# Splitting the first load of a NaN-ignoring row maximum into two loads, over even and odd partitions

## The chip, the cores and the metric

The kernel runs on one core of a Trainium2 chip. The metric is the device time of one execution in microseconds (us), of which the median over several runs is given. A profile is one further execution recorded by the hardware profiler; its engines are called DVE (VectorE), ACT (ScalarE), POOL (GpSimd) and SP (SyncE, which issues the DMAs).

## The reference

The input has 32 x 2048 rows of 2048 float32 values, one in ten of them NaN. The output is the maximum of each row, NaNs left out:

```python
x = np.random.randn(32, 2048, 2048).astype(np.float32)
x[np.random.rand(32, 2048, 2048) < 0.1] = np.nan
return np.nanmax(x, axis=-1).astype(np.float32)
```

The input is 537 MB and is read once; the output is 0.26 MB.

## The kernel before

The 65,536 rows are dealt to 128 partitions, so each partition has 512 rows. They are worked through in 74 tiles. A full tile takes seven rows from every partition (128 x 57,344 bytes, 7168 KB); the first tile, tile 0, takes one row of each partition (128 x 8 KB, 1 MB), and the last tiles are cut into smaller loads. Three buffers `xt0`, `xt1`, `xt2` hold tiles in turn.

Each piece of a tile passes four stages:

1. A load from HBM into `xt`, issued by SP (L269 for tile 0, L466 for all others).
2. ACT reads the upper 16 bits of every value and writes a 16-bit key into a buffer `kt` (L282, `kt<-xt`). The function is a Prelu, whose two slopes send NaN patterns to other keys than numbers.
3. POOL (L292) or, for some pieces, ACT (L282, `xt<-kt`) turns the key back into the upper half of the value in place, which leaves a very low number where a NaN stood.
4. DVE takes the maximum of each row (L299) into `acc`.

Rows of nothing but NaN are found at the end of each part of `acc` (L305, L319), and six stores (L533) bring the result out.

The order of the work is written out by hand. A table `TILES` says how each tile is cut for loads, keys, writing back and maxima. All of it stands in a critical section, in which the class `Order` places the semaphore waits: `order.add` gives an instruction its waits and lets it count up a semaphore. Loads count up one of `LANES = 14` semaphores in turn, and a load waits for the one that used its lane before, and for the DVE maximum that frees its buffer. A full load into a buffer can therefore be issued when the tile three places before it is done.

The critical section starts with a small synchronisation: SP passes it (L276, L582), and ACT and POOL wait for that before their first instructions, ACT's table load and a memset by POOL. The load of tile 0 is issued ahead of the section (`HEADS = 1`): a loop before `tc.tile_critical()` makes its `dma_start` and keeps the instruction in `heads`; inside the section, `order.add` for tile 0 takes this instruction from the list rather than issuing one, so that it gets its lane. The destination is given a dependency offset beyond the buffer (`dep_tracking_offset`), and the instruction is put in `no_tile_sem_insts`, so that the framework adds no waits of its own. The first key pass of ACT (128 x 2048, tile 0) waits for this lane. The loads of tiles 1 and 2 have no earlier user of their buffers and are issued at once after it.

Of the kernel before, what the change touches and what calls it, by code (L numbers as in the profile page):

```python
# [9 lines left out]
D = 2048  # L10

Q = D // 4
# [55 lines left out]
WIDE = 7  # L68
# [5 lines left out]
LEAD = 128  # L74

HEADS = 1

LANES = 14

# [13 lines left out]
def joints(keys, backs, reds):  # L93


    parts = []
    pieces = []
    at = end = step = 0
    for n, wait in backs:
        end += n  # L100
        while at < end:
            at += keys[step]
            step += 1
        if wait is None or wait >= 0:
            parts.append((end - n, end, wait is not None, step + (wait or 0), len(pieces)))
        pieces.append(n)
    needs = []
    done = 0
    for n in map(abs, reds):
        over = [i for i, p in enumerate(parts) if p[0] < done + n and p[1] > done]  # L110
        done += n
        pools = [i for i in over if not parts[i][2]]
        acts = sorted((i for i in over if parts[i][2]), key=lambda i: parts[i][3])
        if pools and acts and parts[pools[-1]][3] > parts[acts[-1]][3]:
            acts = []
        needs.append(pools[-1:] + acts[-1:])
    pairs = {}
    for need in needs:
        if len(need) == 2 and all(sum(i in n for n in needs) == 1 for i in need):
            both = tuple(parts[i][4] for i in need)  # L120
            for i in both:
                pairs[i] = both
    return pairs
# [62 lines left out]
def kernel(  # L186
# [15 lines left out]
    nc = tc.nc  # L202
    P = nc.NUM_PARTITIONS
# [14 lines left out]
    for tiles in GROUPS:  # L218
        at = 0
# [8 lines left out]
    firsts = [  # L228
        nc.alloc_sbuf_tensor(f"xt{i}", [P, WIDE * D], i32).ap() for i in range(HEADS)
    ]  # L230
# [6 lines left out]
    xts = firsts + [  # L237
        sing.tile([P, WIDE * D], i32, name=f"xt{i}") for i in range(HEADS, BUFS)
    ]
# [10 lines left out]
    groups = []  # L250
# [12 lines left out]
    order = Order(nc)  # L263
    heads = []
    for number in range(HEADS):
        (c,) = TILES[number][0]
        gi, base = place[number]
        to = xts[number][:, 0 : c * Q]
        head = nc.sync.dma_start(  # L269
            out=dataclasses.replace(to, dep_tracking_offset=to.offset + P * WIDE * D),  # L270
            in_=groups[gi][0][:, base : base + c * Q],
        )
        tc.no_tile_sem_insts.add(head.ins.name)
        heads.append(head)

    with tc.tile_critical() as section:  # L276

# [52 lines left out]
        lanes = [[] for _ in range(LANES)]  # L330
        turn = 0
# [43 lines left out]
        def freed(*ks):  # L375

            uses = [(back, then, e) for k in ks for back, ((_, then), e) in kfree[k].items()]
            counts = [e[1] for _, _, e in uses if e[0] == "pool"]
            deps = []
            for back, then, e in uses:  # L380
                if back == "act" and order.count["act"] >= then:
                    e = ("act", then)
                if back != "pool" or e[0] == "pool" or all(v < then for v in counts):
                    deps.append(e)
            return deps
# [39 lines left out]
        def find_part(i):  # L425
            gi, lo, hi = spans[i]
            first = groups[gi][2]
            acc = accs[:, first + lo : first + hi]
            deps = [done_at[PARTS[i][2]]]
            if PARTS[i][3] == "dve":  # L430
                none = nones[:, 0 : hi - lo]
                ready[i] = find("dve", nc.vector, deps, acc, none, ALU.bitwise_or)
            else:
                none = late[:, 0 : hi - lo]
                ready[i] = find("pool", nc.gpsimd, deps, acc, none, ALU.add)

        for number, (loads, chunks, reds) in enumerate(TILES):
            keys = [k for ks, _ in chunks for k in ks]
            fresh = {}
            step = 0  # L440
            for ks, bs in chunks:
                assert sum(ks) * Q <= KEYS
                assert sum(ks) == sum(b[0] if isinstance(b, tuple) else b for b in bs)
                fresh[step] = sum(ks) * Q
                step += len(ks)
            backs = [b for _, bs in chunks for b in bs]
            backs = [b if isinstance(b, tuple) else (b, None) for b in backs]
            assert sum(loads) == sum(keys) == sum(b for b, _ in backs) == sum(map(abs, reds))
            pairs[number] = joints(keys, backs, reds)
            for i, part in enumerate(PARTS):  # L450
                if part[3] == number:
                    find_part(i)
            gi, base = place[number]
            xg = groups[gi][0]
            xt, before = xts[number % BUFS], free[number % BUFS]
            assert number < BUFS or state["tile"] > number - BUFS
            landed = []
            at = 0
            for c in loads:
                c *= Q  # L460
                e = order.add(
                    "sp",
                    nc.sync,
                    lambda: heads[number]
                    if number < HEADS
                    else nc.sync.dma_start(  # L466
                        out=xt[:, at : at + c], in_=xg[:, base + at : base + at + c]
                    ),
                    before + lanes[turn],
                    lane=f"load{turn}",  # L470
                    step=16,
                )
                lanes[turn] = [e]
                turn = (turn + 1) % LANES
                landed.append((at, at + c, e))
                at += c
            end = at
            at = lo = part = 0
            for step, c in enumerate(keys):
                c *= Q  # L480
                here = [l for a, b, l in landed if a < at + c and b > at]
                kold = []
                if used + fresh.get(step, 0) > KEYS:
                    key = (key + 1) % NKEYS
                    used = 0
                    assert all(h[3] != key for h in held)
                    assert all(q[2] != key for v in half.values() for q in v)
                    kold = freed(key, (key + 1) % NKEYS) if number in EARLY and at + c == end else freed(key)
                    kfree[key] = {}
                e_key = act(  # L490
                    kold + here,
                    out=kts[key][:, used : used + c],
                    in_=xt[:, at : at + c].bitcast(i16)[:, 1::2],
                    func=ACT.Prelu,
                    bias=EDGE,
                    scale=-1.0,
                    alpha=float(TOP - LOW) / (EDGE - NAN),
                )
                used += c
                at += c  # L500
                for h in held:
                    h[-1] -= 1
                for h in [h for h in held if h[-1] <= 0]:
                    held.remove(h)
                    write(*h[:-1], "act")
                while backs and lo + backs[0][0] * Q <= at:
                    n, wait = backs.pop(0)
                    n *= Q
                    kp = kts[key][:, used - (at - lo) : used - (at - lo) + n]
                    if wait is not None and wait > 0:  # L510
                        held.append([number, lo, lo + n, key, kp, e_key, part, wait])
                    else:
                        who = "pool" if wait is None else "act" if wait == 0 else "dve"
                        write(number, lo, lo + n, key, kp, e_key, part, who)
                    lo += n
                    part += 1
                if number == len(TILES) - 1 and at == end:
                    for h in held:
                        write(*h[:-1], "act")
                    held.clear()  # L520
                maxima(number)
            assert lo == end
# [5 lines left out]
        for (gi, lo, hi), e in zip(spans, ready):  # L528
            _, og, first, _ = groups[gi]
# [4 lines left out]
                    out=og[:, lo:hi], in_=accs[:, first + lo : first + hi].bitcast(i32),  # L534
# [3 lines left out]
                lane="store",  # L538
                step=16,
# [47 lines left out]
```

## Time and profile before

| what | value |
|---|---|
| median of 3 runs | 1251.33 us (1251.32 to 1251.34) |
| the profiled execution | 1251.31 us |
| its span in the profile | 1249.7 us |
| DMA, mean over the span | 430 GB/s |
| busy time of POOL, DVE, ACT | 1158.9, 1109.7, 980.1 us |
| issue of the first load (L269) | at 0.72 us, takes 0.39 us |
| tile 0 usable (first key pass of ACT) | 5.49 us |

The span goes from the first instruction to the last; the execution's time contains 1.6 us around it. In the rows of the profile L269 is a line of the kernel, "xt<-in_x_dram" is what is written and what is read (buffer numbers left out), and "x62" is a count. The DMA figures are of the 16 DMA engines together. A row of the chain of waits has start, length and what ran or was waited for; "issue" is time in which nothing that the profile shows was waited for, and "SPq" is the queue of SP.

### The profile page before, as it was taken

What the parts mean: (1) busy time and instruction counts of PE and PEld (TensorE: products, weight loads), DVE (VectorE), ACT (ScalarE), POOL (GpSimd) and SP (SyncE); (2) the same over time, 40 slices, a digit from 0 to 9 for tenths busy, and PEclk for the clock granted to TensorE, in tenths of its full rate; (3) what the DMA queues carried; (4) which work ended last, traced back from release to release, by engine and by line L of the source; (5) the groups of instructions that cost most, each with busy time, mean ns of one, the idle gap of its engine ahead of it and who ended that gap; (6) DMA issues with size and microseconds to landing.
All of it is one profiled execution on the core that took longest, in us unless ns stands there. A gap on an engine that the chain in (4) does not pass through costs nothing.

```text
span 1249.7 us, 920 instructions
## 1 busy us (share of the span) xinstructions
DVE 1109.7 (89%) x184; ACT 980.1 (78%) x286; POOL 1158.9 (93%) x256
## 2 busy tenths in 40 slices
DVE  0888889888889888888988888988898999999999
ACT  3777777777777777777777777799877799999998
POOL 2999999999999999999999999967999987999998
DMA  9999999999999999999999999999999999999997
GB/s 415 441 428 424 441 441 437 415 441 441 439 426 428 441 439 433 422 439 441 439 426 428 441 439 435 426 433 441 439 428 426 441 437 431 425 436 428 429 428 313
DMA packets 16854, 537.19 MB, mean 430 GB/s; under 512 B 2640, under 2 KB 2640, under 8 KB 5200
## 3 DMA queue, kind: packets, MB, share of 16 engines
q1 hardware_dynamic: 16848, 537.14, 99.5%
q14 instruction: 6, 0.05, 0.0%
HBM read 536.87 MB, written 0.26 MB: 430 GB/s over the span
## 4 chain that ended last, share of the span: by engine, by line
POOL 34%; DVE 30%; DMA 26%; ACT 9%; issue 1%; SPq 0%
POOL xt L292 34%; DVE acc L299 30%; DMA xt<-in_x_dram 26%; ACT kt L282 7%; ACT xt L282 2%; POOL late L305 0%; POOL acc L319 0%; SPq L269 0%; SPq L466 0%; DVE none L305 0%; DVE acc L319 0%; SPq L582 0%; SPq L276 0%
## 5 line engine op out<-in xcount | busy, mean ns | idle before, releaser
L292 POOL TENSOR_SCALAR xt<-kt 128x3584 int16<-128x3584 uint16 (+10 forms) x241 | 1153.9, 4788 | 84.5 <-ACT kt L282 69.3
L299 DVE TENSOR_REDUCE acc<-xt 128x4 f32<-128x8192 f32 (+4 forms) x182 | 1109.4, 6148 | 137.5 <-POOL xt L292 130.6
L282 ACT ACTIVATE kt<-xt 128x3584 uint16<-128x3584 int16 (+10 forms) x252 | 913.9, 3663 | 262.3 <-DMA xt<-in_x_dram 225.0
L282 ACT ACTIVATE xt<-kt 128x512 int16<-128x512 uint16 (+7 forms) x32 | 68.6, 2145 | 0.7
L305 POOL TENSOR_SCALAR late<-acc 128x112 int32<-128x112 f32 (+1 forms) x5 | 2.8, 558 | 0.4
L319 POOL TENSOR_TENSOR acc<-acc,late 128x112 int32<-128x112 int32 (+1 forms) x5 | 2.0, 397 | 0.4
L282 ACT ACT_TABLE_LOAD x1 | 1.3, 1283 | 1.3 <-SPq L276 1.3
L325 POOL MEMSET scalars<- 128x1 f32 x1 | 0.1, 98 | 1.0 <-SPq L276 1.0
L568 POOL MEMSET const-float32-0.0<- 128x1 f32 x1 | 0.1, 98 | 0.2 <-issue 0.2
L282 ACT ACTIVATE scalars<-scalars 128x1 f32<-128x1 f32 x1 | 0.2, 203 | 0.0
L305 DVE TENSOR_SCALAR none<-acc 128x7 int32<-128x7 f32 x1 | 0.2, 169 | 0.0
L319 DVE TENSOR_TENSOR acc<-acc,none 128x7 int32<-128x7 int32 x1 | 0.2, 161 | 0.0
L568 POOL MEMSET const-bfloat16-1.0<- 128x1 bf16 x1 | 0.1, 101 | 0.0
L568 POOL MEMSET const-uint8-127<- 128x1 uint8 x1 | 0.1, 101 | 0.0
L568 POOL MEMSET const-float32-1.0<- 128x1 f32 x1 | 0.1, 98 | 0.0
## 6 DMA issues: line engine op xcount, KB each, us to landing
xt<-in_x_dram SPq DMA_DIRECT2D x62, 7168.0 KB, 22.6
xt<-in_x_dram SPq DMA_DIRECT2D x2, 4096.0 KB, 19.4
xt<-in_x_dram SPq DMA_DIRECT2D x2, 3584.0 KB, 25.6
xt<-in_x_dram SPq DMA_DIRECT2D x5, 1280.0 KB, 29.4
xt<-in_x_dram SPq DMA_DIRECT2D x4, 1536.0 KB, 24.2
xt<-in_x_dram SPq DMA_DIRECT2D x2, 3072.0 KB, 26.3
xt<-in_x_dram SPq DMA_DIRECT2D x1, 5632.0 KB, 19.5
xt<-in_x_dram SPq DMA_DIRECT2D x2, 2816.0 KB, 24.8
```

Of the source, the lines that this page charges most:

```text
L282: lambda: nc.scalar.activation(**kw),
L292: lambda: nc.gpsimd.tensor_scalar(**kw),
L299: return order.add("dve", nc.vector, lambda: do(**kw), deps)
L305: lambda: engine.tensor_scalar(out=none, in0=acc, scalar1=NONE, scalar2=float(0x00800000), op0=ALU.is_equal, op1=ALU.mult,),
L319: lambda: engine.tensor_tensor(out=bits, in0=bits, in1=none, op=op),
L325: e_top = order.add("pool", nc.gpsimd, lambda: nc.gpsimd.memset(top, EDGE), [])
L568: nc = _bacc.Bacc("TRN2", target_bir_lowering=False, num_devices=1)
```

## The change

The load of tile 0 is issued as two loads. The first takes the even partitions (rows 0, 2, 4 ... of `to`), the second the odd ones, 64 rows of 8 KB each. Both are still issued ahead of the critical section, one behind the other on SP. Inside the section each part gets a lane of its own, so tile 0 uses two of the 14 lanes, and all later loads take the next lane in turn. `landed` gets an entry for each part over the same columns, so that ACT's key pass of tile 0 waits for both. No other instruction is changed; the lines below the edit move by a few numbers (the issue of the head stands at L274, that of the other loads at L469).

```diff
+PHASES = ((0, 2), (1, 2))
+
...
-        head = nc.sync.dma_start(
-            out=dataclasses.replace(to, dep_tracking_offset=to.offset + P * WIDE * D),
-            in_=groups[gi][0][:, base : base + c * Q],
-        )
-        tc.no_tile_sem_insts.add(head.ins.name)
-        heads.append(head)
+        heads.append([])
+        for first, step in PHASES:
+            part = to[first::step]
+            head = nc.sync.dma_start(
+                out=dataclasses.replace(
+                    part, dep_tracking_offset=part.offset + P * WIDE * D
+                ),
+                in_=groups[gi][0][first::step, base : base + c * Q],
+            )
+            tc.no_tile_sem_insts.add(head.ins.name)
+            heads[number].append(head)
...
-                e = order.add(
-                    "sp",
-                    nc.sync,
-                    lambda: heads[number]
-                    if number < HEADS
-                    else nc.sync.dma_start(
+                issues = [
+                    lambda: nc.sync.dma_start(
                         out=xt[:, at : at + c], in_=xg[:, base + at : base + at + c]
-                    ),
-                    before + lanes[turn],
-                    lane=f"load{turn}",
-                    step=16,
-                )
-                lanes[turn] = [e]
-                turn = (turn + 1) % LANES
-                landed.append((at, at + c, e))
+                    )
+                ]
+                if number < HEADS:
+                    issues = [lambda head=head: head for head in heads[number]]
+                for issue in issues:
+                    e = order.add(
+                        "sp",
+                        nc.sync,
+                        issue,
+                        before + lanes[turn],
+                        lane=f"load{turn}",
+                        step=16,
+                    )
+                    lanes[turn] = [e]
+                    turn = (turn + 1) % LANES
+                    landed.append((at, at + c, e))
```

## The prediction

> **What bounds the kernel now.** I read the page's strips and queue line first, then the chain of waits that ended last, then the first 25 us of the timeline, and last the busy time of short stretches around the first load.
>
> ```profile
> DVE 1109.7 (89%) x184; ACT 980.1 (78%) x286; POOL 1158.9 (93%) x256
> ...
> DMA  9999999999999999999999999999999999999997
> ...
> q1 hardware_dynamic: 16848, 537.14, 99.5%
> ```
>
> POOL is the busiest compute engine with 93%, but the DMA strip is at nine tenths in every slice but the last: the stream of loads never pauses. The next rows (stretch, its length, busy time and count for DVE, ACT and POOL, clock, DMA share, GB/s) give its pace.
>
> ```profile
> 100.00:1000.00 900.00, 804.16 (x108) 681.93 (x165) 862.83 (x163) 1.00 1.00 434
> 1100.00:1230.00 130.00, 130.00 (x42) 125.41 (x60) 120.48 (x43) 1.00 1.01 430
> ```
>
> A full tile of 7168 KB, that is 7.34 MB, takes 7.34 / 434 = 16.9 us at this pace. So the time at which a tile is usable is the start of the stream plus the bytes ahead of it. The chain of waits says the same from the other side (start, length, what):
>
> ```profile
> 0.72 0.39 SPq L269
> 1.11 0.04 issue
> 1.15 0.01 SPq L276
> 1.17 0.06 issue
> 1.22 0.03 SPq L582
> 1.25 0.13 issue
> 1.38 0.33 SPq L466
> 1.71 0.05 issue
> 1.77 37.60 DMA xt<-in_x_dram
> ...
> 1032.58 22.14 DMA xt<-in_x_dram
> 1054.72 0.02 issue
> ...
> 1068.06 0.02 issue
> 1068.08 169.86 DVE acc L299 x52
> 1237.94 0.01 issue
> 1237.95 8.93 DVE acc L299 x4
> ```
>
> It begins at the very instruction that the change splits (L269), goes through the second full tile, which lands at 1.77 + 37.60 = 39.37, comes back to loads up to the landing at 1054.72, and ends in DVE without a gap from 1068.08 on. The load that lands at 1054.72 was issued 22.14 us before, 5.2 us more than the 16.9 us its bytes need, so it queued behind the load before it: the stream, not its issue, set that landing. Hence whatever moves the start of the stream by d moves the end by d. I take this one to one. A chain shows the last releaser alone, and POOL at 93% could have a second chain almost as late; but POOL's data come from the same stream, so it moves along.
>
> **The change part by part.** The head load (tile 0, 128 rows of 8 KB, 1.05 MB) becomes two loads of 64 rows each, 0.52 MB. It adds one DMA issue on SP, one semaphore lane used at the start, and one wait on ACT, whose first key pass now needs both parts.
>
> (1) The added issue on SP. Its price is the duration of an issue:
>
> ```profile
> L269 SPq DMA_DIRECT2D xt<-in_x_dram x1: 385/385/385, 0.7 to 0.7; - x1
> L466 SPq DMA_DIRECT2D xt<-in_x_dram x2: 333/376/420, 1.4 to 1.8; - x2
> ```
>
> These are minimum, median and maximum in ns, of L466 those before 2 us; a 64-row issue is not in the trace, and I take 0.39 us, between 0.33 and 0.42. Everything that SP has behind it moves by that: the entry of the critical section (L276, L582), for which ACT and POOL wait, and the first two L466 issues, from 1.38 to about 1.77 and from 1.77 to 2.16.
>
> ```profile
> 1.34 1.28 ACT L282 ACT_TABLE_LOAD   x1 [1.34 <-SPq L276]
> 1.38 0.10 POOL L325 MEMSET scalars<- 128x1 f32 x1 [0.95 <-SPq L276]
> ...
> 2.63 0.20 ACT L282 ACTIVATE scalars<-scalars 128x1 f32<-128x1 f32 x1
> 5.49 1.91 ACT L282 ACTIVATE kt<-xt 128x2048 uint16<-128x2048 int16 x1 [2.65 <-DMA xt<-in_x_dram]
> 7.49 2.46 POOL L292 TENSOR_SCALAR xt<-kt 128x2048 int16<-128x2048 uint16 x1 [6.01 <-ACT kt L282]
> 9.98 2.29 DVE L299 TENSOR_REDUCE acc<-xt 128x1 f32<-128x2048 f32 x1 [9.98 <-POOL xt L292]
> 22.48 3.19 ACT L282 ACTIVATE kt<-xt 128x3584 uint16<-128x3584 int16 x1 [15.09 <-DMA xt<-in_x_dram]
> ```
>
> ACT then idles 2.65 us until the head lands, so a table load that is 0.39 us later costs nothing; POOL idles 6.01 us. For the L466 issue, look at the DMA engines. The next rows count a packet's bytes where it starts:
>
> ```profile
> 1.70:1.80 0.10, 0.00 (x0) 0.10 (x1) 0.00 (x0) 1.00 1.91 328
> 1.80:1.90 0.10, 0.00 (x0) 0.10 (x1) 0.00 (x0) 1.00 1.40 246
> 1.90:2.00 0.10, 0.00 (x0) 0.10 (x1) 0.00 (x0) 1.00 1.40 246
> 2.00:2.10 0.10, 0.00 (x0) 0.10 (x1) 0.00 (x0) 1.00 1.33 246
> 2.10:2.20 0.10, 0.00 (x0) 0.10 (x1) 0.00 (x0) 1.00 1.18 246
> 2.20:2.45 0.25, 0.00 (x0) 0.25 (x1) 0.00 (x0) 1.00 0.00 0
> ...
> 2.45:4.45 2.00, 0.00 (x0) 0.37 (x2) 0.00 (x0) 1.00 0.99 418
> ...
> 4.60:4.70 0.10, 0.00 (x0) 0.00 (x0) 0.00 (x0) 1.00 4.85 2048
> ...
> 5.10:5.20 0.10, 0.00 (x0) 0.00 (x0) 0.00 (x0) 1.00 1.33 573
> ```
>
> The first bytes of the head start at 1.7, about 1.0 us after its issue began, and the first large packets of tile 1 (the jump to 2048 GB/s) at 4.6. An issue at 1.77 would be ready at 1.77 + 1.0 = 2.8, with 1.8 us in hand: hidden. If that cover were gone, the price would be the 0.39 us. The second part is issued at 1.11, ready at about 2.1, and wanted only when the first part's 0.52 MB are through, at about 1.7 + 0.3 + 0.52/0.418 = 3.3 us: hidden too, with 1.1 us in hand.
>
> (2) The extra wait on ACT and the 14 lanes. Tile 0 needs nothing early: its chain ends at 9.98 + 2.29 = 12.27 and lets the third full load be issued, whose bytes are wanted only when the second full tile is through, at about 39. Cost nothing, with 26 us in hand. Each load still waits for the one 14 before it; the names shift by one, the distance does not.
>
> (3) One more set of completion writes. 16848 packets are 117 loads and stores of 144, that is 128 rows and 16 completions; the split adds 16, one to each engine. The rows of the pace above bound it: with 54 issues in 900 us the stream makes 434 GB/s, with 40 in 130 us 430, so 130 x (1 - 430/434) = 1.2 us over 40 issues, at most 0.03 us each, and down to 0. I take 0.02 us.
>
> (4) The start of the 16 engines. Between 1.70 and 2.20 the rows add up to 1312 GB/s x 0.1 us = 131 KB, 16 packets of 8 KB, and nothing starts in the next 0.25 us: one first packet for each of 16 engines, spread over 0.4 to 0.5 us. At 4.60 to 5.20 tile 1's first packets are spread by as much, so the delay of the late engines is carried along, and a tile is usable when the last engine is done. If an engine gets its list after those ahead of it got theirs, lists of half the rows halve the spread: 0.45 / 2 = 0.22 us earlier for the last one. The ends of the range are 0 (spread set by a step per engine, not per row) and 0.45 (spread gone). No row excludes a loss here; that is rival two. I take 0.15 us, since what counts is the last engine at 1054.72, and by then small delays over 60 tiles may have made another engine the last.
>
> Sum: +0 (issue) + 0 (wait, lanes) + 0.02 - 0.15 = -0.13 us. The profiled execution took 1251.31 us (span 1249.7, the rest around it), the median of the runs shown is 1251.33. So 1251.31 - 0.13 = 1251.18, in round figures 1251.2 us. The bound for a difference, 0.2%, is 2.50 us here, about what a measurement of this kernel can tell from no change, and more than this change can win.
>
> A rule that speaks against the edit: the Trainium skill, "DMA: Bandwidth & Descriptors", Rules for kernel authors, says of two transfers to disjoint partition halves "Don't bother", because both use the same 16 engines, and advises one 128-partition transfer. The trace agrees as to the pace (418 GB/s in one load leaves little to win), and by this rule the sum is rival one's.
>
> **Rivals.** One: nothing is won. The spread is per engine or does not last, or the last engine at 1054.72 is one that started early. For it: the spread is 0.45 us of a 1251 us run. Against: it is still there 3 us later, at tile 1's first packets. Time 1251.33 with 0 to 0.03 us added, 1251.3.
>
> Two, slower: engines collide on every other partition. All loads of this trace span 128 adjacent partitions, so none shows how 64 spaced ones are dealt to engines. If two engines meet at one place, both parts go at half of 418 GB/s, and the 1.05 MB cost 2.5 us more, all of it at the head of the stream: 1251.31 + 2.5 = 1253.8. From a pace just below 209 GB/s on it is slower by over 0.2%; if one part alone is hit it is 1252.6. Nothing in the trace speaks for it but that it was never tried. The Trainium skill, "SBUF — State Buffer", Door 1: The DMA port swizzle, gives the pace by how many of 16 ports the partitions reach; every other partition reaches all 16, so by that page the pace stays; no run here shows it.
>
> Three, a little slower: the issue is not hidden. If the second issue stalls until the first part's lists are done and pushes tile 1's past 4.6, a gap opens in the stream. Against it: the 1.8 us in hand. Price 0.1 to 0.6 us, the upper end a 0.42 us issue with 0.2 us of gap behind it: 1251.4 to 1251.9, say 1251.7.
>
> **How the numbers follow.** Forecast 0.55 at 1251.2 (1250.85 to 1251.3 by the ends of step 4); rival one 0.20 at 1251.3; rival three 0.12 at 1251.7; rival two 0.09, a third of it at or past the bound; 0.04 for what I do not see, such as another interleaving of packets that changes the pace, split over all three signs. The likeliest gives 1251.2. The range 1250.8 to 1252.6 takes the whole spread as gain and the collision of one part as loss; it leaves out the full collision and half of the unseen, under 1 in 10. Faster by over 0.2%: 0.02; slower: 0.03 + 0.02 = 0.05; within: 0.93.
>
> **What would show it.** Two issues at the head's line and q1 with 16864 packets show the edit. Step 1: the first load of the loop issued near 1.8, no stretch without DMA before 5. Step 2: the head's key pass still far ahead of 22. Step 4: first packets that are all started before about 2.0 instead of 2.2, ACT's first full key pass before 22.4 and the second tile's landing before 39.37. Rival two: well under 418 GB/s in 2.45 to 4.45 and tile 1 past 23.5. The prediction is wrong if the landing at 39.37 moves by one amount and the end by another: then step "one to one" fails.

## The result and the profile after

The changed kernel takes 1252.76 us in the median of 22 executions (1252.02 to 1253.60), the kernel before 1251.34 us (1251.27 to 1251.92, 22 executions beside them). The ratio is 1.0012, with a 95% interval of 1.0006 to 1.0017: slower by 1.4 us, clear of no change, though by less than 0.2%. The forecast was 1251.2 us, range 1250.8 to 1252.6. The ranges of the two kernels do not overlap, and the changed one scatters more. On some chips of the later experiments the kernel before itself scattered over more than 1 us; there the medians say little, and the profiles and the lowest times are used.

The profiled execution took 1252.67 us, 1.36 us more than the one before. First the page of the changed kernel, engines and DMA queue:

```profile
DVE 1109.7 (89%) x184; ACT 980.1 (78%) x286; POOL 1159.7 (93%) x256
...
q1 hardware_dynamic: 16864, 537.14, 99.4%
```

Busy times are those of before within 0.8 us, and there are the 16 more packets. So the time went into when things start. The chain of waits of the changed kernel (start, length, what):

```profile
0.72 0.56 SPq L274
1.28 0.06 issue
1.33 0.57 SPq L274
1.91 0.04 issue
1.96 0.01 SPq L283
...
2.19 0.35 SPq L469
2.54 0.06 issue
2.59 38.30 DMA xt<-in_x_dram
...
1033.86 22.12 DMA xt<-in_x_dram
1055.97 0.02 issue
...
1069.36 178.78 DVE acc L306 x56
```

The two issues of the head take 0.56 and 0.57 us, where the whole head took 0.39. The second full tile lands at 2.59 + 38.30 = 40.89, not 39.37: 1.52 us later. The landing near 1055, from which DVE runs to the end without a gap, moves from 1054.72 to 1055.97, 1.25 us. The timeline of the changed kernel shows the steps between:

```profile
2.15 1.28 ACT L289 ACT_TABLE_LOAD   x1 [2.15 <-SPq L283]
6.33 1.91 ACT L289 ACTIVATE kt<-xt 128x2048 uint16<-128x2048 int16 x1 [2.69 <-DMA xt<-in_x_dram]
24.00 3.19 ACT L289 ACTIVATE kt<-xt 128x3584 uint16<-128x3584 int16 x1 [15.76 <-DMA xt<-in_x_dram]
```

Tile 0 is usable 0.84 us later (6.33 against 5.49), tile 1 1.52 us later (24.00 against 22.48), and after that nothing is added. The DMA engines of the changed kernel in short stretches (the last column is GB/s, the one ahead of it the DMA share):

```profile
1.90:2.00 0.10, 0.00 (x0) 0.00 (x0) 0.00 (x0) 1.00 0.00 0
2.00:2.10 0.10, 0.00 (x0) 0.00 (x0) 0.00 (x0) 1.00 0.77 164
2.10:2.20 0.10, 0.00 (x0) 0.05 (x1) 0.02 (x1) 1.00 1.51 328
2.20:2.45 0.25, 0.00 (x0) 0.25 (x1) 0.08 (x1) 1.00 1.10 262
...
2.45:4.45 2.00, 0.00 (x0) 1.19 (x2) 0.00 (x0) 1.00 0.92 336
```

The first packets start after 2.00, not after 1.70; by the packet records the very first starts at 2.07, not at 1.74. Up to 2.45 they are 164 x 0.1 + 328 x 0.1 + 262 x 0.25 = 115 KB, 14 packets of 8 KB, so the spread over the engines is still about 0.45 us. The three parts of the loss at tile 1 are thus about 0.33 us of late start (2.07 - 1.74), about 0.5 us inside tile 0 (0.84 - 0.33) and 0.7 us at the change to tile 1 (1.52 - 0.84).

The trace also has the completion that each of the 16 engines posts for a load. For the second full tile they lie within 0.56 us of each other before and within 1.47 us after; their mean is 0.80 us later, their last 1.52. One or a few engines are far behind the rest.

### The profile page after: what moved, and what is told of

The parts are those of the page before. It is cut to its first block, busy times and chain, and to the rows that moved or that the text cites. A ratio compares the mean times of both kernels' runs of the same rounds, so it can differ in the third digit from the quotient of the medians.

```text
span 1250.9 us, 922 instructions
## 1 busy us (share of the span) xinstructions
DVE 1109.7 (89%) x184; ACT 980.1 (78%) x286; POOL 1159.7 (93%) x256
## 3 DMA queue, kind: packets, MB, share of 16 engines
q1 hardware_dynamic: 16864, 537.14, 99.4%
## 4 chain that ended last, share of the span: by engine, by line
POOL 40%; DVE 28%; DMA 23%; ACT 8%; issue 1%; SPq 0%
POOL xt L299 40%; DVE acc L306 28%; DMA xt<-in_x_dram 23%; ACT kt L289 6%; ACT xt L289 2%; POOL late L312 0%; SPq L274 0%; POOL acc L326 0%; SPq L469 0%; DVE none L312 0%; DVE acc L326 0%; SPq L593 0%; SPq L283 0%
```

## The experiments

Eighteen kernels ran in five groups, each group on one chip with the kernel before beside it. "Tile 2 usable" is the landing of the second full tile in the chain of waits (39.37 before). Differences are to the kernel before of the same group, whose median stands once for each group; there are 11 executions of each kernel. The 95% interval of one such ratio is about 0.0009 to both sides, 1.1 us, so single differences under that stand on the ranges and on repeats.

| kernel | tile 2 usable | profiled | median (range) | before: median (range) | difference of medians, of lowest |
|---|---|---|---|---|---|
| column halves | 40.64 | 1252.35 | 1252.35 (1251.82 to 1252.99) | 1251.70 (1251.33 to 1252.68) | +0.65, +0.49 |
| adjacent halves | 41.44 | 1253.66 | 1253.75 (from 1253.39) | the same | +2.05, +2.06 |
| head inside the section | 39.66 | 1252.93 | 1252.43 (1251.66 to 1253.01) | the same | +0.73, +0.33 |
| tile 10 split | 39.47 | 1252.60 | 1251.85 (1251.50 to 1252.85) | the same | +0.15, +0.17 |
| tile 1 late | 39.97 | 1251.51 | 1251.88 (1251.50 to 1252.55) | 1251.46 (1251.28 to 1251.71) | +0.42, +0.22 |
| column quarters | 41.54 | 1254.07 | 1252.89 (1252.16 to 1254.07) | the same | +1.43, +0.88 |
| change, tiles 1 and 2 ahead | 40.03 | 1252.23 | 1252.44 (1251.82 to 1254.17) | the same | +0.98, +0.54 |
| change, second time | 41.12 | 1252.56 | 1252.39 (1252.07 to 1253.56) | the same | +0.93, +0.79 |
| spare load behind the head | 39.57 | 1252.82 | 1252.07 (1251.65 to 1253.19) | 1252.43 (1251.25 to 1253.12) | -0.36, +0.40 |
| tile 1 in halves | 39.40 | 1252.60 | 1251.66 (1251.36 to 1252.68) | the same | -0.77, +0.11 |
| column halves, tiles 1 and 2 ahead | 39.26 | 1251.49 | 1251.82 (1251.48 to 1253.09) | the same | -0.61, +0.23 |
| no split, tiles 1 and 2 ahead | 39.38 | 1251.92 | 1251.44 (1251.25 to 1252.60) | the same | -0.99, 0.00 |
| column halves, second time | 39.56 | 1251.59 | 1252.03 (1251.53 to 1252.96) | 1251.46 (1251.32 to 1251.63) | +0.57, +0.21 |
| column halves ahead, second time | 39.52 | 1251.63 | 1252.02 (1251.45 to 1252.78) | the same | +0.56, +0.13 |
| tile 1 later still | 39.55 | 1251.46 | 1251.56 (1251.44 to 1251.86) | the same | +0.10, +0.12 |
| change, tiles ahead, second time | 40.80 | 1252.08 | 1252.31 (1251.97 to 1253.35) | the same | +0.85, +0.65 |
| change, third time | 41.09 | 1253.99 | 1253.20 (1252.07 to 1254.60) | 1251.93 (1251.21 to 1252.80) | +1.27, +0.86 |
| no split, tiles ahead, second time | 39.31 | 1252.25 | 1252.14 (1251.25 to 1253.26) | the same | +0.21, +0.04 |

### Which split is it: rows or columns, spaced or adjacent

My first theory, P, blamed the 64 spaced rows; its rival, S, two loads at the cold start, whatever their shape. Two column halves keep all 128 partitions in each load:

```diff
-PHASES = ((0, 2), (1, 2))
+PHASES = ((0, 2 * Q), (2 * Q, 4 * Q))
-            part = to[first::step]
+            part = to[:, lo_at:hi_at]
```

> The first load in two parts again, but each over all 128 partitions and half of the columns (128 x 4 KB). Theory P (the partitions: 64 spaced rows take longer to issue, 0.57 us against 0.39, and leave some of the 16 engines late): the issues take 0.33 to 0.45 us each, the first packets start at 1.7, the second full tile is usable at 39.4 as before, time 1251.3 to 1251.5. Theory S (two loads at the cold start of the stream, whatever their shape, leave some engines without work for a moment): the second full tile is usable near 40.9, time 1252.0 to 1253.6.

The head's issues in this kernel (minimum, median and maximum in ns), and then its chain:

```profile
L274 SPq DMA_DIRECT2D xt<-in_x_dram x2: 372/396/420, 0.7 to 1.1; - x2
```

```profile
1.84 0.33 SPq L469
...
2.23 38.41 DMA xt<-in_x_dram
```

The issues and the first packets (1.73 us) are those of 128 rows, as P had it, and yet the second full tile lands at 40.64, as S had it. Each theory seems to hold one half; but this is one profile, and in the repeat further down the same kernel lands at 39.56. The next kernel takes adjacent partitions, `PHASES = (slice(0, 64), slice(64, 128))`:

> The first load in two parts over partitions 0 to 63 and 64 to 127. Theory P: if it is the spacing of the partitions, the issues are back at 0.39 us and the time at 1251.3 to 1251.7; if it is the number of 64 rows, issue and time stay as in the changed kernel (0.57 us, 1252 to 1253.6); if half of the partitions can be reached at half the pace only, 2.45 to 4.45 us runs at 210 GB/s and the time is 1253.8. Theory S: 1252.0 to 1253.6 with issues of 0.39 us.

Its issues, and its DMA engines in two stretches:

```profile
L274 SPq DMA_DIRECT2D xt<-in_x_dram x2: 568/572/575, 0.7 to 1.3; - x2
```

```profile
3.45:4.45 1.00, 0.00 (x0) 0.20 (x1) 0.00 (x0) 1.00 1.01 213
...
5.20:6.00 0.80, 0.00 (x0) 0.00 (x0) 0.00 (x0) 1.00 1.19 246
```

(The table's range has no upper end for this kernel because two of its executions took 1398 and 1453 us, which nothing here explains.) Two things follow. At the head, the long issue comes with loads of 64 rows, spaced or not, and not with two loads of 128 rows. And 64 adjacent partitions run at 213 GB/s, about half pace, while the spaced ones do not. The same stretch of the changed kernel, and below it of the changed kernel's second profile and of the kernel before:

```profile
3.45:4.45 1.00, 0.00 (x0) 0.20 (x1) 0.00 (x0) 1.00 0.95 369
```

```profile
3.45:4.45 1.00, 0.00 (x0) 0.20 (x1) 0.00 (x0) 1.00 1.01 418
```

```profile
3.45:4.45 1.00, 0.00 (x0) 0.00 (x0) 0.00 (x0) 1.00 1.06 451
```

At 418 GB/s with a share of 1.01 the spaced rows do not collide; 369 comes with a share of 0.95, that is in part with idle engines. The Trainium skill, "SBUF — State Buffer", Door 1: The DMA port swizzle, has partitions 0 to 63 reach 8 of 16 ports, with an asymptote of about 218 GB/s. The trace agrees: 213 GB/s were measured. The 246 of the later stretch doesn't speak against it, because its share of 1.19 shows packets that run on past its end; per full share it is 246 / 1.19 = 207 GB/s, an estimate.

### Is a late start passed on, and does the split cost in mid-stream

`HEADS = 0` in the kernel before issues the head inside the section:

> The first load whole, but issued inside the critical section (no load ahead of it): its issue moves from 0.72 to about 0.98 to 1.1 us and nothing else changes. If a delay at the start of the stream reaches the end one to one, the second full tile is usable 0.25 to 0.4 us later than 39.39 and the time is 1251.6 to 1251.8. If the end is not tied to the start, 1251.3.

The chain of this kernel:

```profile
0.94 0.39 SPq L466
...
1.85 37.81 DMA xt<-in_x_dram
```

The issue moved by 0.22 us, the second full tile by 0.29. The expected time was missed: the median is 1252.43 us, but it is no measure on this chip (see the last runs), and the lowest execution is 0.33 us above the lowest before. This agrees with a late start that is passed on. It doesn't show it cleanly: in this profile eight of the 16 engines also start about half a microsecond after the others, which further down is seen with the head of the kernel before too.

For the split in mid-stream, tile 10 is loaded in even and odd rows:

```diff
+                phases = PHASES if number in SPLIT else ((0, 1),)   # SPLIT = (10,)
+                for first, step in phases:
...
+                            out=xt[first::step, at : at + c],
+                            in_=xg[first::step, base + at : base + at + c],
```

> The first load whole as before; the full load of tile 10, in the middle of the running stream, is issued in two parts over the even and the odd partitions (64 rows of 56 KB each). Theory P: if 64 spaced rows are dealt to the engines so that these hinder each other, the stream falls below 434 GB/s for this tile, to about 340 GB/s as at the head of the changed kernel, and the time is 1254 to 1256. If only the longer issue and the late lists count, they are covered by the tile in flight: 1251.3 to 1251.5. Theory S: no cold start here, 1251.3 to 1251.5.

Its issues between 130 and 160 us, its stretch from 157 us on, and the same stretch of the kernel before:

```profile
L472 SPq DMA_DIRECT2D xt<-in_x_dram x3: 328/564/592, 135.3 to 152.8; - x3
```

```profile
157.00:174.00 17.00, 15.29 (x3) 12.45 (x3) 16.71 (x4) 1.00 1.00 432
```

```profile
157.00:174.00 17.00, 15.27 (x3) 12.45 (x3) 16.71 (x4) 1.00 1.00 435
```

The 64-row issues are as long here, up to 0.59 us, but under the tile in flight they cost nothing that shows: the landing after the split tile is at 191.79 (191.69 before), 0.10 late, as the second full tile already was (39.47). So P's collision is out.

### Is it that tile 1's list comes late

Theory L: with two head loads tile 1 is issued later (2.19 us in the changed kernel, 1.84 with column halves, 1.38 before), and engines run empty at the end of tile 0. Theory N: it is the number of loads. First, the head whole and tile 1's load behind ACT's warm-up operation:

```diff
-        act([e_top], out=warm, in_=top, func=ACT.Prelu, alpha=0.5)
+        e_warm = act([e_top], out=warm, in_=top, func=ACT.Prelu, alpha=0.5)
...
-                    before + lanes[turn],
+                    before + lanes[turn] + ([e_warm] if number == 1 else []),
```

> The first load whole, as before, but the load of tile 1 waits for ACT's warm-up operation, so that it is issued at about 2.85 us, not at 1.38. Its first packet would be ready near 3.9 us, still 0.7 us before the head is through at 4.6. Theory L (the engines read ahead, and a list for tile 1 that comes late leaves some of them empty at the change from tile 0 to tile 1): the second full tile is usable later than 39.39, by 0.3 to 1.5 us, and the time rises as much. Theory N (it is the number of loads at the start that matters): 39.4 and the time of the kernel before.

With it ran the head in four column parts (`PHASES` of four times `Q` columns), the change with `HEADS = 3`, which puts the unsplit loads of tiles 1 and 2 ahead of the section, and the change again:

> The first load in four parts over the columns (128 x 2 KB each), so that tile 1 is issued at about 2.65 us. Theory N: more loads, more loss: the second full tile is usable at 41 or later, and the time is above that of the two column halves (1252.35) by 0.5 us or more. Theory L: the same sign, through the later issue of tile 1, landing and time as in the run with the late issue of tile 1. If neither holds, 40.6 as with two halves.

> The changed kernel (even and odd partitions), with the loads of tiles 1 and 2, unsplit, issued ahead of the critical section too, right behind the second part: tile 1 at about 1.95 us, not 2.19. Theory L: some of the loss comes back, the second full tile usable 0.2 to 0.6 us before that of the changed kernel on this chip. Theory N: no difference.

> The changed kernel once more, beside the others on one chip: issues of 0.57 us, first packets at 2.05 to 2.1, second full tile usable between 40.3 and 41.2, 1252.0 to 1253.6 us.

With the late issue (2.85 us) tile 2 landed at 39.97 and the median rose by 0.42 us, for L. The quarters cost 1.43 us. The change with the earlier issue of tile 1 (1.96 us) landed 1.1 us sooner than the change beside it (40.03 against 41.12), but took the same time, 1252.44 against 1252.39: against L. One profile is one draw of something that scatters. The chain of this kernel also corrects the first section. Its third issue is tile 1's whole load, 128 rows, directly behind the second part:

```profile
1.96 0.59 SPq L274
```

It takes 0.59 us, in the repeat 0.58. With column halves in front of it, the same issue takes 0.42. So the rows of a load alone don't set the length of its issue; what does is open.

The next four kernels were meant to separate the two theories:

> The first load whole, and behind it, ahead of the critical section, a second load of 128 x 512 B of the same data into a spare buffer that nothing reads (64 KB, 0.15 us of the stream); ACT's first key pass waits for both. Theory N (one load more between the first load and tile 1 disturbs the start, whatever it carries): the second full tile is usable 0.5 to 1.3 us later than 39.39, time 0.4 to 1.0 us above the kernel before. Theory L (only tile 1's later issue counts, 1.84 against 1.38): at most 0.2 + 0.15 us. If the size of the parts counts and not their number: 0.15 us.

> The first load whole; tile 1's load in two halves over the columns (128 x 28 KB each), issued at 1.38 and about 1.8. Theory N in its wide form (more loads near the cold start): 0.4 to 1.0 us above the kernel before. Theory L, and theory N in its narrow form (the loads between tile 0 and tile 1): tile 1's first list is in time, nothing changes, 39.4 and within 0.2 us of the kernel before.

> The first load in two column halves as before, with the unsplit loads of tiles 1 and 2 ahead of the critical section: tile 1 at about 1.6 us, not 1.84. Theory L: the loss of the column halves (0.5 to 0.65 us) shrinks to 0.2 to 0.3. Theory N: it stays at 0.5 to 0.65.

> No split; the loads of tiles 0, 1 and 2 all ahead of the critical section: tile 1 issued at about 1.15 us, not 1.38. If late lists for tile 1 are what costs, there is nothing to win where the kernel before has no empty engine, and fewer slow executions where it has: 0 to 0.2 us below the kernel before. Otherwise the same time.

The spare load (`spare`, 128 x 512 B) leaves tile 2 0.20 us late, 0.15 of which are its own bytes; tile 1 in halves (`[14, 14]`, not `[28]`) leaves tile 2 at 39.40; the column halves with tiles 1 and 2 ahead (tile 1 issued at 1.63) land at 39.26, 0.11 us before the kernel before. The medians decide nothing here, because that of the kernel before is 1252.43. L looked right, and N looked wrong as far as the spare load goes. So the column kernels were repeated on one chip, with a later issue of tile 1 still (behind five warm-up operations) and the change with tiles ahead:

> The two column halves again, now on one chip with the next three; tile 1 issued at about 1.84 us. Theory L (an engine whose next list comes late runs empty and pays the first latency again): some of tile 1's first packets take 2300 ns and more instead of 2116, second full tile 0.3 to 1.3 us later than 39.39, time 0.4 to 0.7 us above the kernel before. If the first result was that chip's own disturbance: 39.4 and the time of the kernel before.

> The two column halves with tiles 1 and 2 ahead of the section, tile 1 issued at about 1.63 us. Theory L: second full tile at 39.2 to 39.4, time within 0.2 us of the kernel before, and 0.3 us or more under the run without the two loads ahead. If the earlier issue is not what counts: the same time as that run.

> The first load whole; tile 1's load waits for five warm-up operations of ACT, not one, so that it is issued at 3.3 to 3.7 us, not 2.85. Theory L: all engines now run empty at the end of tile 0, second full tile at 40.4 to 41.0, time 0.9 to 1.5 us above the kernel before. Otherwise it grows by no more than the 0.2 us or so of its predecessor.

> The changed kernel with tiles 1 and 2 ahead of the section, again. If the 64-row lists alone cost (0.33 us in the first packets) and the engines no longer run empty, 0.3 to 0.5 us above the kernel before; as it stood the first time, 0.9 to 1.0.

Here L falls. The chain of the kernel with the latest issue of tile 1:

```profile
3.23 0.34 SPq L468
3.56 0.05 issue
3.62 35.93 DMA xt<-in_x_dram
```

Issued 1.85 us later than before, tile 1 costs 0.10 us (1251.44 to 1251.86 against 1251.32 to 1251.63), where 0.9 to 1.5 were expected; the column halves take 1252.03 and 1252.02 us with tile 1 at 1.84 and at 1.63; and the change is no better for the earlier issue: +0.98 beside +0.93 on one chip, +0.85 on this one.

N is left, but it isn't shown. For it: the kernel before had 1251.46 us on two chips; on one of them two column parts cost 0.57 and 0.56 us, on the other four cost 1.43. Against it: the two column profiles here land at 39.56 and 39.52 and took 1251.59 and 1251.63 us, so three of the four profiles of column halves show next to no loss; and the single head load with tile 1 issued at 2.85 us had +0.42 as well. The parts also differ in more than their number. By the packet records a packet takes 309 ns at 8 KB, 159 at 4 KB and 84 at 2 KB in the median. For 1 MB on 16 engines that is 2.47, 2.54 and 2.69 us, an estimate: 0.07 us of the loss of the halves and 0.2 us of that of the quarters would be pace.

One thing here needs no second load. The stretch from 1.70 to 2.20 us, in which the first packets start, in the kernel before, with tile 1 issued at 2.85 us, and with it issued at 3.23:

```profile
1.70:2.20 0.50, 0.00 (x0) 0.50 (x1) 0.00 (x0) 1.00 1.44 262
1.70:2.20 0.50, 0.00 (x0) 0.50 (x1) 0.00 (x0) 1.00 1.06 131
1.70:2.20 0.50, 0.00 (x0) 0.50 (x1) 0.00 (x0) 1.00 1.89 246
```

That is 16, 8 and 15 packets of 8 KB, with the same head load and an issue of 0.37 to 0.39 us in all three. In the middle one the other eight start between 2.47 and 2.82 us. So its landing at 39.97 can come from the start of tile 0 and needn't come from tile 1's issue. The packet records show such a late half in five of the twenty profiles, two with one head load (tile 1 late, head inside the section) and three with two (the change the second time, column halves the second time, column halves ahead the second time); all 16 engines are then busy 0.4 to 0.6 us later than in the others. Why it happens is open.

The last two runs:

> The changed kernel a third time, beside the next. If the mean engine sets the floor of the loss and one late engine the rest: lowest execution 0.5 to 0.8 us above the lowest of the kernel before, median 0.8 to 1.4, the engines' ends of the second full tile 0.6 to 0.9 us later on the mean.

> No split, the loads of tiles 0, 1 and 2 all ahead of the critical section, again. If it is a better kernel than the one before: 0.1 us or more below it in the median on a quiet chip. If its lead was the other chip's disturbance: the same time within 0.1 us.

The change is slower in all three measurements, by 1.42, 0.93 and 1.27 us in the median and 0.75, 0.79 and 0.86 in the lowest execution. The engines' mean in the second full tile was 0.80, 0.72 and 1.49 us late in the three profiles, so the expected 0.6 to 0.9 failed in the profile for which it was written, and the lowest execution lies just above the expected 0.5 to 0.8. The loads of all three tiles ahead of the section are no better than the kernel before (+0.21 median, +0.04 lowest); no kernel here beats it.

What the three chips with a scattering kernel before (medians 1251.70, 1252.43 and 1251.93) add can be seen in the chains. In eight of their ten profiles the chain goes through one more landing behind the one near 1055, and in no other profile. Here it is without any split, in the second run with tiles 1 and 2 ahead:

```profile
1032.66 22.12 DMA xt<-in_x_dram
...
1109.46 22.53 DMA xt<-in_x_dram
...
1247.84 0.18 DVE none L305
```

The first landing is at 1054.78, as before; DVE's closing operation L305 starts 193.06 us after it, where the kernel before has 192.18 (1246.90 - 1054.72). With the spare load it is 193.44, with the head inside the section 193.33, in the third profile of the change 193.08; in all profiles on the other chips it is 192.2. So up to 1.3 us are lost at the end of the stream on these chips, whatever the head, and their medians mix both losses.

**What this settles.** The change costs 0.9 to 1.4 us in the median and 0.75 to 0.86 in the lowest execution, in three measurements of three (the third on a chip that also loses time at the end). About 0.33 us of that is seen at the first packets: they start at 2.07 us with spaced rows, at 2.08 with adjacent ones, and at 1.73 with two loads of 128 rows. That tile 1 is issued later is not the cause (+0.10 us at 3.23). In mid-stream the split costs nothing that shows.

**What stays open** is the larger rest, which the first profile puts inside tile 0 and at the change to tile 1. That two loads in an empty stream cost about 0.56 us of their own is likely by the medians, and no more. The sum 0.33 + 0.56 = 0.89 is near the 0.93 of one chip, but below the 1.42 and 1.27 of the others, and the interval of each median difference is 1.1 us to both sides. One late engine doesn't explain the rest: the last engine is 0.46 us behind the next in the first profile (1.42 us lost) and 1.00 us in the second (0.93 lost). That the engines wait for something between the loads is only argued from idle stretches in the trace. Nor is it clear why the spare load, also a second one, showed almost nothing at the start of its profile, or why the single load issued at 2.85 us has +0.42 in the median when its profile has +0.05.

## Why the prediction was wrong

- **What bounds the kernel: right.** The loss is made in the first 24 us and the rest of the run repeats it. "One to one" held roughly for the first link (0.22 us in, 0.29 out, in a profile with a scattered start) and for the last: a landing near 1055 that is 1.25 us late gave 1.36 us, in the quarters 2.72 (1057.44) gave 2.61 (1254.07 - 1251.46). Between them it holds less well: 1.52 us at 39.37 was 1.25 at 1054.72, and in the second profile of the change 1.75 was 1.16, so by the sign that the prediction named this step is not exact. A likely reason, not shown, is that the last engine of an early tile need not be the last one later.
- **Step 1 failed, in two ways.** The price of the issue, 0.39 us between 0.33 and 0.42, was taken from 128-row loads; it is 0.57. And the step asked only what the added issue delays, not what stands ahead of the first part's own packets. Those had no cover: they start at 2.07 and not at 1.74. Of these 0.33 us, 0.17 are the longer issue, and 0.16 pass between its end and the first packet (0.79 us, before 0.63). That tile 1's issue is hidden was right: the issue at 3.23 cost 0.10.
- **Step 2 was right.** ACT's first pass still idles 2.69 us ahead of its data, and tile 0 is usable 17.7 us before tile 1.
- **Step 3 was right** in its count (16864) and the tile 10 run shows no cost in a running stream. Its price, 0.02 us, was taken from the running stream; at the start a second load may cost about 0.56 us (likely, not shown), and no row of the trace before has two loads in an empty stream.
- **Step 4 failed.** The spread of the first packets did not halve: 14 of 16 in 0.45 us. The 0.15 us gain that decided the sign is not there. The one landing of a split head that was earlier (39.26, column halves) was 39.52 in the repeat. Instead of -0.13 us the sum came to +1.42, of which the runs show 0.33 in step 1; the rest is open.
- **Rival one** (nothing won) had the right view of step 4. **Rival two** is real, but for adjacent halves: 213 GB/s, 1253.75 us, almost the 1253.8 worked out. That the two numbers are so close is partly luck, as this kernel also starts 0.34 us late (2.08). For the change it does not hold. The sign I named for it, a pace under 418 and tile 1 past 23.5, appeared (336 and 24.00) through the late start and idle engines: a sign that two mechanisms share tells nothing. **Rival three** was nearest, an issue that isn't hidden; but it was tile 1's issue that it took to be late, and its 0.1 to 0.6 us lacked the higher price of the short loads (0.57, not 0.42) and the part that stays open.
- The rule of the Trainium skill quoted in the prediction, "DMA: Bandwidth & Descriptors", Rules for kernel authors ("Don't bother"), pointed the right way, and the trace goes beyond it: at the head of an empty stream the split costs 0.9 to 1.4 us.

## What to carry to other kernels

The first load of a stream has no cover, so its issue must be priced for itself, not by the rows of other loads; a load of fewer partitions can take longer to issue. A split that is free in a running stream (tile 10: nothing that shows) can cost about 1 us at the head of an empty one. Where the end follows the last of 16 engines, an average pace hides the loss: look at when the last one is done. And one profile is one draw: the same head load had all 16 engines busy at 2.82 us in one profile and at 2.2 in two others.

## What the hardware showed that was not expected

- An issue of a 64-row load takes 0.56 to 0.59 us, at the head and in mid-stream, adjacent or spaced. Most issues of a 128-row load ahead of the run's last 80 us take 0.33 to 0.44, with 2 KB to 56 KB per row. Exceptions are a 128-row load directly behind two 64-row loads (0.58 and 0.59) and tile 2's load behind the two halves of tile 1 (0.64).
- 64 adjacent partitions load at 213 GB/s in the stretch from 3.45 to 4.45 us, 64 spaced ones at 369 to 418 GB/s in the same stretch.
- In five of twenty profiles eight of the 16 engines start their first packets late, so that all 16 are busy 0.4 to 0.6 us later than in the other profiles, with one head load or with two.
- The executions of the change scatter over 1252.02 to 1253.60 us where those of the kernel before stay within 1251.27 to 1251.92. It isn't shown that the second load causes it: single head loads with another place of issue scatter over 1 us too (1251.50 to 1252.55 with tile 1 late, beside 1251.28 to 1251.71).
- On three of five chips of the experiments up to 1.3 us are lost behind 1055 us in eight of ten profiles, with a split head and without (193.06 us from that landing to L305, unsplit, against 192.18).
